# Last projection and final norm in pieces of 384 and 128 tokens, with the final products two tiles at a time

## The chip, the cores and the metric

The kernel runs on one core of one Trainium2 chip. The metric is the device time of one execution in microseconds (us). A core has a matrix engine (PE; its weight loads are shown apart as PEld), a vector engine (DVE), a scalar engine (ACT), a general engine (POOL) and a queue engine (SP) that issues the transfers (DMAs). Each engine runs its own instruction list strictly in order; semaphores join them. Every matmul has its weight load (LDWEIGHTS) ahead of it.

## The reference

A two-layer encoder over 512 tokens with 1024 features, in float32. Layer 0 mixes with differential attention and a gated linear recurrence, layer 1 with a spatial gating unit; each layer ends with a SwiGLU feed-forward. What matters here is the end:

```python
def rms_norm(x, gain):
    xf = x.astype(jnp.float32)
    y = xf * lax.rsqrt(jnp.mean(xf * xf, axis=-1, keepdims=True) + EPS)
    return (y * gain.astype(jnp.float32)).astype(x.dtype)

def swiglu(h, w_in, w_out):
    gate, up = jnp.split(h @ w_in, 2, axis=-1)
    return (jax.nn.silu(gate) * up) @ w_out
...
        h = h + swiglu(rms_norm(h, norm_ffn[l]), w_ffn_in[l], w_ffn_out[l])
    return rms_norm(h, norm_final)
```

## The kernel before, in words

The state `h` lies transposed on the chip: 8 feature tiles of 128 partitions by 512 tokens, two tiles to a buffer (`hs[0]` to `hs[3]`). A product takes its float32 operands as two rounded parts, high and low (type fp32r), and forms three matmuls for each pair of blocks: high by high, high by low, low by high. They accumulate in a PSUM tile of up to 512 tokens.

The program is not written in the order in which it runs. Every step is recorded as an operation with an engine, an estimated cost in us and the buffers that it reads and writes (`Plan.op`, L80). `Plan.schedule` (L110) then plays the whole program through with these costs: whenever an engine is free in that model, it takes the ready operation of lowest priority number for which buffer slots are free. The order of these starts is the order in which instructions are issued on each engine. So a cost that is changed anywhere can move operations anywhere, and on the chip an engine keeps the order even where the real times differ from the costs. `vtt` records a DVE step, `gtt` a POOL step, `act` an ACT step, `mms` a group of matmuls, all through helper lines (L298, L310, L322, L329), so the profile's rows are told apart by their tiles.

The feed-forward (`ffn`, L982) makes 22 gated tiles in groups of 2, 4, 4, 4, 4, 4. `one` (L995) adds the product of one group with the output weights for one feature tile `d`. For all groups but the last of layer 1 it runs over all 512 tokens (tiles `fo_...`). The last group, four tiles (`g18b` and `g20b` hold two each), is projected by the code at the end (L1099 to L1138): a loop `e` over two halves of the tokens, in each a loop over the 8 feature tiles. One pass of the inner loop is 4 x 3 = 12 matmuls into a PSUM tile `last` (there are four such slots), a DVE subtraction into `h` (the weights are laid out so that the product is subtracted), a square on ACT (`sq_fin`), the sum of the first seven squares on POOL, and a scaling of `h` by the gain on ACT. After the 8 tiles, the two squares tiles are summed over the features by matmuls with one column (`st_fin`, plain float32, two rows of the trace for each matmul), DVE forms mean plus epsilon (`ms_fin`), POOL takes the power -1/2 (`rr_fin`), DVE puts that on a diagonal (`dg_fin`), a matmul spreads it over all partitions (`sp_fin`), DVE multiplies each tile of `h` by it, and SP sends the result out in five DMAs for each half.

Earlier in the program the same kind of norm stands in layer 1 (`rstat`, L417; tiles `st_m`, `ms_m`, `rr_m`, `rp_m`, `dg_m`, `sp_m`), between the products `vo` of the spatial gating unit; `wlo` is the low part of a weight tile there.

Of the kernel before, what the change touches and what calls it, by code (L numbers as in the profile page):

```python
# [24 lines left out]
GROUPS = (2, 4, 4, 4, 4, 4)
H = S // 2
# [188 lines left out]
def encoder_kernel(  # L215
# [21 lines left out]
    nc = tc.nc  # L237
    V, A, G, T = nc.vector, nc.scalar, nc.gpsimd, nc.tensor
# [32 lines left out]
    plan = Plan(kinds, limits)  # L271
# [33 lines left out]
    def vts(o, a, s0, s1, op0=ALU.mult, op1=ALU.add, cost=0.07):  # L305
        return plan.op("DVE", cost, lambda: V.tensor_scalar(use(o), use(a), use(s0), use(s1), op0, op1),
                       [o], [a, s0, s1])

    def gtt(o, a, b, op, cost=1.25, prio=None):
        return plan.op("POOL", cost, lambda: G.tensor_tensor(use(o), use(a), use(b), op), [o], [a, b], prio=prio)  # L310
# [8 lines left out]
    def act(o, a, func, scale=1.0, bias=0.0, accum=None, cost=0.52, table=None, prio=None):  # L319
        def fn():  # L320
            kw = {} if accum is None else {"accum_out": use(accum)}
            A.activation(use(o), use(a), func, bias=use(bias), scale=use(scale), **kw)  # L322
        outs = [o] if accum is None else [o, accum]
        return plan.op("ACT", cost, fn, outs, [a, bias, scale], table=table, prio=prio)

    def mms(ps, items, after=(), cost=None):
        def fn():
            for o, l, r, s0, s1 in items:
                T.matmul(use(o), lhsT=use(l), rhs=use(r), start=s0, stop=s1)  # L329
        ins = [x for it in items for x in it[1:3]]  # L330
        return plan.op("PE", cost if cost is not None else 0.2315 * len(items), fn, [ps], ins, after=after)

    colt = cst.tile([P, 50], F32, name="colt")
    ident = cst.tile([P, P], F32, name="ident")
    ones = cst.tile([P, 1], F32, name="ones")
    mhalf = cst.tile([P, NB], F32, name="mhalf")
    onesf = cst.tile([P, P], F32, name="onesf")
# [233 lines left out]
    for i in range(2):  # L571
        ps = buf("aux", f"u{i}")
# [268 lines left out]
    d0 = da_proj(0)  # L841
    gla_core(3, r3, vi)
    d1 = da_proj(1)
# [7 lines left out]
    for h in range(NB):  # L851
        ps = project(we[28 + h], xs0, f"g{h}")
# [8 lines left out]
    hs = [buf("big", f"h{j}") for j in range(KC // 2)]  # L861
# [120 lines left out]
    def ffn(l, norm, name, finish, after=()):  # L982
        gs, k0 = [], 0

        def quad(q, n, k0):
            i = weights[0]
            weights[0] += 1
            pr = -1e6 + i * 10
            raw = buf("hraw", f"raw{i}", shape=(P, 4, n * P))
            off = 4 * P * k0  # L990
            hdma(raw, wfo[l, q, :, off:off + 4 * n * P].rearrange("p (d c) -> p d c", d=4), 256 * n, pr)
            return [rounded(raw(lambda ap, e=e: ap[:, 2 * e:2 * e + 2]), (P, 2, n * P), f"{e}_{i}", pr,
                            lo_cost=0.06 + n * 0.27, hi_cost=0.09 + n * 0.22) for e in range(2)]

        def one(d, wt, ps, n, gs, cols=None):  # L995
            cut = (lambda ap: ap) if cols is None else (lambda ap: ap[:, cols:cols + H])
            o = ps(cut if cols is None else (lambda ap: ap[:, :H]))
            hi, lo = wt
            for k in range(n):
                wh, wl = (b(lambda ap, k=k: blk(ap[:, d % 2], k)) for b in (hi, lo))  # L1000
                xh, xl = (View(g.buf, g.part, lambda ap, g=g: cut(g.fn(ap))) for g in gs[k])
                mms(ps, [(o, wh, xh, k == 0, False), (o, wh, xl, False, False), (o, wl, xh, False, k == n - 1)],
                    cost=0.7 if cols is None else 0.36)

        def out(dp, wts, n, gs, last):
            for d in (2 * dp, 2 * dp + 1):
                ps = buf("aux", f"fo{d}_{k0}{name}")
                one(d, wts, ps, n, gs)
                hd = row(hs[d // 2], d % 2)
                o = vtt(hd, hd, ps, ALU.subtract)  # L1010
                if last:
                    finish(hd)
                    marks.append(o)

        prev, k0 = None, 0
        m = 0
        for gi, n in enumerate(GROUPS):
            cur, store = [], None
            wts = {}
            for i in range(n):  # L1020
                y = gated(l, m, norm, name, after if m < 3 else ())
                if i % 2 == 0:
                    store = buf("huge", f"g{m}{name}", F32R)
                split_pair(store, y, 2 * (i % 2))
                cur.append(pair(store, 2 * (i % 2)))
                m += 1
                if prev:
                    if i % 2 == 0:
                        wts = dict(zip((i, i + 1), quad(i // 2, prev[1], prev[2])))
                    out(i, wts[i], prev[1], prev[0], False)  # L1030
            prev = (cur, n, m - n)
        gs, n, k0 = prev
        wts = quad(0, n, k0) + quad(1, n, k0)
        return gs, n, wts, one, out
# [4 lines left out]
    gs, n, wts, one, out_pair = ffn(0, n1, "a", n2.add, after=[da_end[3]])  # L1039
# [18 lines left out]
    for hf in range(2):  # L1058
        ps = project_natural(wov[hf], n2.xs, f"vo{hf}")
# [17 lines left out]
    for g in range(KC):  # L1077
        ps = project(wo[g], n2.xs, f"uo{g}")
# [13 lines left out]
        b, i = mxs[g - g % 2], 2 * (g % 2)  # L1092
# [5 lines left out]

    fin = [None, None]  # L1099
    gs, n, wts, one, _ = ffn(1, n3, "b", None)  # L1100
    for e in range(2):
        for d in range(KC):
            ps = buf("aux", f"last{d}{e}")
            one(d, wts[d // 2], ps, n, gs, e * H)
            hv = hs[d // 2](lambda ap, d=d, e=e: ap[:, d % 2, e * H:(e + 1) * H], part=(d % 2, e))
            vtt(hv, hv, ps(lambda ap: ap[:, :H]), ALU.subtract, cost=0.34)
            sq = buf("tmp", f"sq_fin{d}{e}")
            sv = sq(lambda ap: ap[:, :H])
            act(sv, hv, AF.Square, cost=0.35)
            if d == 0:  # L1110
                fin[e] = sq
            elif d < KC - 1:
                f = fin[e](lambda ap: ap[:, :H])
                gtt(f, f, sv, ALU.add, cost=0.7)
            act(hv, hv, AF.Copy, scale=colt[:, 4 * KC + d:4 * KC + d + 1], cost=0.4)
        st = buf("aux", f"st_fin{e}")
        for i, x in enumerate((fin[e], sq)):
            for t in range(2):
                mms(st, [(st(lambda ap, t=t: ap[:, t:t + 1]), x(lambda ap, t=t: blk(ap, t)), ones,
                          i == 0 and t == 0, i == 1 and t == 1)], cost=0.28)  # L1120
        ms, rr = buf("ms", f"ms_fin{e}"), buf("rr", f"rr_fin{e}")
        vts(ms(lambda ap: ap[:, 0:2]), st(lambda ap: ap[:, 0:2]), 1.0 / D, EPS)
        gtt(rr(lambda ap: ap[:, 0:2]), ms(lambda ap: ap[:, 0:2]), mhalf[:, 0:2], ALU.pow, cost=0.6)
        dg = buf("trn", f"dg_fin{e}")
        vtt(dg(lambda ap: ap[:, 0, :H].rearrange("p (b c) -> p b c", b=2)),
            ident.rearrange("p (b c) -> p b c", b=1).broadcast_to([P, 2, P]),
            rr(lambda ap: ap[:, 0:2].rearrange("p (b c) -> p b c", c=1).broadcast_to([P, 2, P])), ALU.mult, cost=0.34)
        sp_ = buf("aux", f"sp_fin{e}")
        sv = sp_(lambda ap: ap[:, :H])
        mms(sp_, [(sv, onesf, dg(lambda ap: ap[:, 0, :H]), True, True)], cost=0.45)  # L1130
        for d0, d1 in ((0, 1), (1, 2), (2, 4), (4, 6), (6, 8)):
            j, i, n_ = d0 // 2, d0 % 2, d1 - d0
            for d in range(d0, d1):
                v = hs[d // 2](lambda ap, d=d, e=e: ap[:, d % 2, e * H:(e + 1) * H], part=(d % 2, e))
                vtt(v, v, sv, ALU.mult, cost=0.34)
            plan.op("DMA", n_ * 128 / 360, lambda d0=d0, d1=d1, j=j, i=i, n_=n_, e=e: nc.sync.dma_start(
                out[d0:d1, :, e * H:(e + 1) * H].rearrange("a p c -> p a c"),
                hs[j].ap()[:, i:i + n_, e * H:(e + 1) * H]), [], [hs[j](part=(x, e)) for x in range(i, i + n_)])  # L1138

    with tc.manual_schedule(engines={ENG.PE, ENG.DVE, ENG.Activation, ENG.Pool, ENG.SP}):  # L1140
        for o in plan.schedule():
# [80 lines left out]
```

## Time and profile before

| | |
|---|---|
| median of 3 runs | 1203.88 us (1202.47 to 1203.91) |
| profiled execution, own time | 1204.61 us |
| its span, first to last instruction | 1202.80 us |
| PE busy | 1163.3 us, 97% of the span |
| DVE busy | 915.4 us, 76% |
| ACT busy | 579.1 us, 48% |
| POOL busy | 188.0 us, 16% |
| granted PE clock, mean | 0.995 |

The profile is one execution. Its busy share of PE tells that nearly the whole span is matmuls one behind the other; where something else sets the time is seen by stage, in the chain of waits and in the timeline. A matmul's own duration includes the way through the array, and the next starts before it ends, so what a matmul costs in a stream is the distance between starts.

### The profile page before, as it was taken

How to read it: one execution, taken by the hardware profiler on the slowest of the kernel's cores; microseconds unless marked ns; L12 is line 12 of the kernel's file. 1: busy time of each engine (PE TensorE's matmuls, PEld its weight loads, DVE VectorE, ACT ScalarE, POOL GpSimd, SP SyncE). 2: the span in 40 equal slices, each digit the busy share in tenths (PEclk: the TensorE clock that was granted, in tenths of full speed). 3: DMA queues.
4: the chain of work that ended last, by engine and by line, in shares of the span. 5: the costliest groups of instructions: out<-in, count | busy, mean ns of one | idle time of the engine just before them, and what ended most of it. 6: DMA issues, size and time to landing. Idle time of an engine off the chain costs nothing.

```text
span 1202.8 us, 17650 instructions
## 1 busy us (share of the span) xinstructions
PE 1163.3 (97%) x7072; PEld 1031.0 (86%) x7072; DVE 915.4 (76%) x1304; ACT 579.1 (48%) x881; POOL 188.0 (16%) x185
## 2 busy tenths in 40 slices
PE   6989999999999999999999999999999999999997
PEld 3868888778778999999999888878899999999996
DVE  5467698769697997777777873757799778877874
ACT  5244465657554544444444444335555444444444
POOL 4355584213130000000000040003000000000003
PEclk9989999999999999999999999999999999999998
DMA  6420420343415232424233423330333232323302
GB/s 217 165 82 1 111 81 10 91 123 88 158 35 174 81 106 70 141 71 141 71 140 106 141 78 98 88 105 5 148 110 133 71 132 79 108 102 106 105 1 71
DMA packets 28686, 118.58 MB, mean 99 GB/s; under 512 B 5272, under 2 KB 7448, under 8 KB 20412
## 3 DMA queue, kind: packets, MB, share of 16 engines
q1 hardware_dynamic: 28604, 117.46, 29.5%
q8 instruction: 55, 0.90, 0.3%
q14 instruction: 27, 0.22, 0.1%
HBM read 115.30 MB, written 4.23 MB: 99 GB/s over the span
## 4 chain that ended last, share of the span: by engine, by line
PE 80%; DMA 7%; DVE 6%; issue 4%; ACT 2%; POOL 1%; SPq 0%; POOLq 0%; DVEq 0%; ACTq 0%
PE fo_0b L329 8%; PE fo_0a L329 8%; PE uo L329 4%; PE oo L329 4%; PE vo L329 3%; PE lv L657 2%; DMA raw<-wev 2%; PE fo_18a L329 2%; PE vi L329 2%; PE last L329 1%; PE q L329 1%; PE zf L329 1%; PE zb L329 1%; PE oe L329 1%; DMA xin<-xT 1%
## 5 line engine op out<-in xcount | busy, mean ns | idle before, releaser
L298 DVE TENSOR_TENSOR wlo<-raw,whi 128x1024 fp32r<-128x1024 f32 (+1 forms) x65 | 85.4, 1314 | 29.5 <-ACT whi L317 29.4
L298 DVE TENSOR_TENSOR lb<-comb,hb 128x1024 fp32r<-128x1024 f32 x44 | 53.7, 1220 | 38.5 <-ACT hb L317 38.5
L317 ACT CAST whi<-raw 128x1024 fp32r<-128x1024 f32 (+1 forms) x65 | 66.8, 1031 | 22.3 <-DMA raw<-wev 10.7
L298 DVE TENSOR_TENSOR la<-raw,ha 128x1024 fp32r<-128x1024 f32 x44 | 55.0, 1249 | 27.1 <-ACT ha L317 26.9
L317 ACT CAST hb<-comb 128x1024 fp32r<-128x1024 f32 x44 | 46.1, 1048 | 59.7 <-PE pa9a L948 2.4
L310 POOL TENSOR_TENSOR sq_m<-sq_m,sq_m 128x512 f32<-128x512 f32 x12 | 19.9, 1657 | 328.9 <-ACT sq_m L322 328.4
L317 ACT CAST ha<-raw 128x1024 fp32r<-128x1024 f32 x44 | 46.2, 1049 | 48.8 <-PE pa10a L948 2.4
L298 DVE TENSOR_TENSOR l<-raw,h 128x1024 fp32r<-128x1024 f32 (+1 forms) x48 | 54.5, 1136 | 17.0 <-ACT h L317 15.4
L317 ACT CAST hc<-comb 128x1024 fp32r<-128x1024 f32 x44 | 46.1, 1047 | 37.3 <-PE fo_0b L329 15.5
L298 DVE TENSOR_TENSOR comb<-comb,raw 128x512 f32<-128x512 f32 x88 | 62.4, 709 | 0.1
L317 ACT CAST h<-raw 128x1024 fp32r<-128x1024 f32 (+1 forms) x48 | 46.6, 975 | 27.9 <-PE pb4b L948 2.0
L310 POOL TENSOR_TENSOR sq_fin<-sq_fin,sq_fin 128x256 f32<-128x256 f32 x12 | 8.9, 738 | 327.2 <-ACT sq_fin L322 326.8
L687 POOL TENSOR_TENSOR W<-W,T 128x512 f32<-128x512 f32 x38 | 52.7, 1394 | 39.7 <-PE lv L657 35.5
L298 DVE TENSOR_TENSOR lc<-comb,hc 128x1024 fp32r<-128x1024 f32 x44 | 54.7, 1244 | 2.2 <-ACT hc L317 2.2
L924 DVE TENSOR_TENSOR comb<-raw 128x1024 f32<-128x1024 f32 x44 | 54.7, 1243 | 0.0
L329 PE MATMUL vo<-whi,x_m 128*128 128x512 f32 x128 | 40.3, 391 | 0.1
L329 PE MATMUL uo<-x_m,whi 128*128 128x512 f32 x128 | 40.1, 394 | 0.0
L329 PE MATMUL oo<-mx,whi 128*128 128x512 f32 x128 | 39.6, 390 | 0.0
L657 PEld LDWEIGHTS lv<-W,km 128*128 128x128 f32 x224 | 31.4, 196 | 8.6 <-ACT km L650 6.2
L317 ACT CAST hd<-raw 128x512 fp32r<-128x512 f32 x44 | 27.4, 622 | 22.4 <-PE pa0a L948 2.0
L657 PE MATMUL lv<-W,km 128*128 128x128 f32 x224 | 32.5, 290 | 5.8 <-ACT km L650 5.8
L310 POOL TENSOR_TENSOR sq_f<-sq_f,sq_f 128x512 f32<-128x512 f32 x12 | 20.2, 1686 | 103.1 <-ACT sq_f L322 103.1
(2624 smaller groups left out, 4208.7 us busy)
## 6 DMA issues: line engine op xcount, KB each, us to landing
raw<-wfi SPq DMA_DIRECT2D x44, 1024.0 KB, 4.9
raw<-wfo SPq DMA_DIRECT2D x20, 1024.0 KB, 4.9
raw<-we SPq DMA_DIRECT2D x23, 512.0 KB, 5.2
raw<-wev SPq DMA_DIRECT2D x8, 512.0 KB, 12.4
raw<-woe SPq DMA_DIRECT2D x8, 512.0 KB, 3.8
raw<-wov SPq DMA_DIRECT2D x8, 512.0 KB, 3.7
raw<-wo SPq DMA_DIRECT2D x8, 512.0 KB, 3.6
raw<-woo SPq DMA_DIRECT2D x8, 512.0 KB, 3.7
```

The source lines that it names most:

```text
L298: return plan.op("DVE", cost, lambda: V.tensor_tensor(use(o), use(a), use(b), op), [o], [a, b], prio=prio, after=after, alt=alt, port=insi ...
L310: return plan.op("POOL", cost, lambda: G.tensor_tensor(use(o), use(a), use(b), op), [o], [a, b], prio=prio)
L317: return plan.op("ACT", cost, lambda: A.copy(use(o), use(a)), [o], [a], prio=prio)
L329: T.matmul(use(o), lhsT=use(l), rhs=use(r), start=s0, stop=s1)
L657: T.matmul(blk(ps.ap(), b), lhsT=blk(km.ap(), b), rhs=mixed(0, b * P, P, s)(W.ap()), start=True, stop=True)
L687: return lambda: eng.tensor_tensor(view(W.ap()), view(W.ap()), fn(TT.ap()), ALU.mult)
L924: plan.op("DVE", 1.14, lambda: V.tensor_tensor(comb.ap()[:, 0:2], raw.ap()[:, 0:1].broadcast_to([P, 2, S]), raw.ap()[:, 1:3], ALU.add), [c ...
```

## The change

The two halves become a piece of 384 tokens and a piece of 128 tokens. The squares are summed on DVE and no longer on POOL. The final multiplication takes two feature tiles with one DVE instruction, and the output leaves in four DMAs for each piece in place of five. The costs given to the scheduler become formulas of the width; for the 512-token products of both feed-forwards that gives 0.70072 in place of 0.7 for each block.

```diff
-        def one(d, wt, ps, n, gs, cols=None):
-            cut = (lambda ap: ap) if cols is None else (lambda ap: ap[:, cols:cols + H])
-            o = ps(cut if cols is None else (lambda ap: ap[:, :H]))
+        def one(d, wt, ps, n, gs, c0=0, w=S):
+            cut = lambda ap: ap[:, c0:c0 + w]
+            o = ps(lambda ap: ap[:, :w])
...
-                    cost=0.7 if cols is None else 0.36)
+                    cost=0.03 + w * 0.00131)
...
-    for e in range(2):
+    for e, (c0, w) in enumerate(((0, 3 * P), (3 * P, P))):
+        nb = w // P
+        cw = lambda ap, w=w: ap[:, :w]
         for d in range(KC):
             ps = buf("aux", f"last{d}{e}")
-            one(d, wts[d // 2], ps, n, gs, e * H)
-            hv = hs[d // 2](lambda ap, d=d, e=e: ap[:, d % 2, e * H:(e + 1) * H], part=(d % 2, e))
-            vtt(hv, hv, ps(lambda ap: ap[:, :H]), ALU.subtract, cost=0.34)
+            one(d, wts[d // 2], ps, n, gs, c0, w)
+            hv = hs[d // 2](lambda ap, d=d, c0=c0, w=w: ap[:, d % 2, c0:c0 + w], part=(d % 2, e))
+            vtt(hv, hv, ps(cw), ALU.subtract, cost=0.06 + w * 0.00105)
...
             elif d < KC - 1:
-                f = fin[e](lambda ap: ap[:, :H])
-                gtt(f, f, sv, ALU.add, cost=0.7)
-            act(hv, hv, AF.Copy, scale=colt[:, 4 * KC + d:4 * KC + d + 1], cost=0.4)
+                f = fin[e](cw)
+                vtt(f, f, sv, ALU.add, cost=0.06 + w * 0.00105)
+            act(hv, hv, AF.Copy, scale=colt[:, 4 * KC + d:4 * KC + d + 1], cost=0.2 + w * 0.0008)
         st = buf("aux", f"st_fin{e}")
         for i, x in enumerate((fin[e], sq)):
-            for t in range(2):
+            for t in range(nb):
...
-        for d0, d1 in ((0, 1), (1, 2), (2, 4), (4, 6), (6, 8)):
-            j, i, n_ = d0 // 2, d0 % 2, d1 - d0
-            for d in range(d0, d1):
-                v = hs[d // 2](lambda ap, d=d, e=e: ap[:, d % 2, e * H:(e + 1) * H], part=(d % 2, e))
-                vtt(v, v, sv, ALU.mult, cost=0.34)
-            plan.op("DMA", n_ * 128 / 360, lambda d0=d0, d1=d1, j=j, i=i, n_=n_, e=e: nc.sync.dma_start(
-                out[d0:d1, :, e * H:(e + 1) * H].rearrange("a p c -> p a c"),
-                hs[j].ap()[:, i:i + n_, e * H:(e + 1) * H]), [], [hs[j](part=(x, e)) for x in range(i, i + n_)])
+        for j in range(KC // 2):
+            v = lambda ap, c0=c0, w=w: ap[:, :, c0:c0 + w]
+            plan.op("DVE", 0.06 + w * 0.0021, lambda j=j, v=v, sp_=sp_, w=w: V.tensor_tensor(
+                v(hs[j].ap()), v(hs[j].ap()),
+                sp_.ap()[:, :w].rearrange("p (a c) -> p a c", a=1).broadcast_to([P, 2, w]), ALU.mult),
+                [hs[j](part=(x, e)) for x in range(2)], [sp_], prio=1e6 + len(plan.ops))
+            plan.op("DMA", w / 360, lambda j=j, v=v, c0=c0, w=w: nc.sync.dma_start(
+                out[2 * j:2 * j + 2, :, c0:c0 + w].rearrange("a p c -> p a c"), v(hs[j].ap())),
+                [], [hs[j](part=(x, e)) for x in range(2)])
```

What stands where now, at the places that the prediction speaks of. In these rows the number behind a tile's name tells buffers apart; `h_2550`, `h_2562`, `h_2573` and `h_2587` are `hs[0]` to `hs[3]`.

On DVE, the end of the second half before, from the subtraction of the last tile (`last_11050`) to the multiplications:

```order
L298 TENSOR_TENSOR h_2587<-h_2587,last_11032 128x256
L298 TENSOR_TENSOR h_2587<-h_2587,last_11050 128x256
L306 TENSOR_SCALAR ms_fin_11079<-st_fin_11073 128x2
L298 TENSOR_TENSOR dg_fin_11083<-ident,rr_fin_11081 128x256
L298 TENSOR_TENSOR h_2550<-h_2550,sp_fin_11085 128x256 x2
```

The same place now; `sp_fin_10974` belongs to the piece of 384, the other tiles to the piece of 128, whose last subtraction is that of `last_11038`:

```order
L298 TENSOR_TENSOR h_2587<-h_2587,last_11019 128x128
L298 TENSOR_TENSOR h_2587<-h_2587,last_11038 128x128
L298 TENSOR_TENSOR sq_fin_10944<-sq_fin_10944,sq_fin_11047 128x128
L1136 TENSOR_TENSOR h_2587<-h_2587,sp_fin_10974 128x2x384
L298 TENSOR_TENSOR sq_fin_10944<-sq_fin_10944,sq_fin_11062 128x128
L306 TENSOR_SCALAR ms_fin_11074<-st_fin_11071 128x1
L298 TENSOR_TENSOR dg_fin_11078<-ident,rr_fin_11076 128x128
L1136 TENSOR_TENSOR h_2550<-h_2550,sp_fin_11080 128x2x128
```

Between the last subtraction and the statistics DVE now has three instructions, one of them a product of the other piece with 768 elements in each partition.

On PE, in the first tiles of the last projection before: the first matmul that reads the second pair of `g20b` is that of `last_10754` in the last row, behind the second and third block of the fourth tile, `last_10792`.

```order
L329 MATMUL last_10792<-g18b,h_130_10714 128x256 x2
L329 MATMUL last_10792<-g18b,l_130_10728 128x256
L329 MATMUL last_10792<-g20b,h_130_10714 128x256 x2
L329 MATMUL last_10792<-g20b,l_130_10728 128x256
L329 MATMUL last_10754<-g20b,h_130_10676 128x256 x2
```

The same place now:

```order
L329 MATMUL last_10794<-g18b,h_130_10714 128x384 x2
L329 MATMUL last_10794<-g18b,l_130_10728 128x384
L329 MATMUL last_10754<-g20b,h_130_10676 128x384 x2
L329 MATMUL last_10754<-g20b,l_130_10691 128x384
L329 MATMUL last_10770<-g20b,h_130_10676 128x384 x2
```

Ahead of that matmul stood 36 of 256 tokens, three blocks for each of four tiles; now there are 30 of 384 tokens, since the fourth tile has only one block there.

On DVE in the norm of layer 1, between the products `vo` (minus before, plus now):

```order
-L306 TENSOR_SCALAR ms_m_6528<-st_m_6518 128x4
-L298 TENSOR_TENSOR wlo_6535<-raw_6436,whi_6523 128x1024
-L428 CAST rp_m_6546<-rr_m_6530 128x4
-L298 TENSOR_TENSOR rp_m_6546<-rr_m_6530,rp_m_6546 128x4
-L298 TENSOR_TENSOR dg_m_6551<-ident,rp_m_6546 128x512 x2
+L306 TENSOR_SCALAR ms_m_6523<-st_m_6515 128x4
+L428 CAST rp_m_6535<-rr_m_6525 128x4
+L298 TENSOR_TENSOR wlo_6540<-raw_6436,whi_6530 128x1024
+L298 TENSOR_TENSOR rp_m_6535<-rr_m_6525,rp_m_6535 128x4
+L298 TENSOR_TENSOR dg_m_6546<-ident,rp_m_6535 128x512 x2
```

The weight step `wlo` has gone behind the first step that needs POOL's result. On PE both groups of that norm, `st_m` and `sp_m`, stand three `vo` matmuls earlier than before. Up to there, and between there and the end of the program, the instructions on every engine stand as before.

## Rows read from the trace of the kernel before

**Rows 1.** Chain of waits, 1150 to 1203 us: start, us, what, rows merged
```profile
1163.46 4.12 PE fo_0b L329 x18
...
1172.14 8.41 PE last L329 x68
1180.55 0.78 PE st_fin L329 x8
1181.34 2.26 PE last L329 x18
1183.60 0.43 PE sp_fin L329 x2
1184.03 6.84 PE last L329 x57
```

**Rows 2.** Timeline behind the last projection: start, us, engine, line, what, [idle before <- releaser]
```profile
1192.01 0.28 PE L329 MATMUL last<-g20b,l 128*128 128x256 f32 x1
1192.33 0.42 DVE L298 TENSOR_TENSOR h<-h,last 128x256 f32<-128x256 f32 x1 [1.02 <-PE last L329]
1192.69 1.17 PE L329 MATMUL st_fin<-ones,sq_fin 128*128 128x1 f32 x8 [0.40 <-POOL sq_fin L310]
1192.79 0.42 ACT L322 ACTIVATE sq_fin<-h 128x256 f32<-128x256 f32 x1 [0.48 <-DVE h L298]
1193.90 0.16 DVE L306 TENSOR_SCALAR ms_fin<-st_fin 128x2 f32<-128x2 f32 x1 [1.15 <-PE st_fin L329]
1194.14 0.71 POOL L310 TENSOR_TENSOR rr_fin<-ms_fin,mhalf 128x2 f32<-128x2 f32 x1 [1.50 <-DVE ms_fin L306]
1194.88 0.42 DVE L298 TENSOR_TENSOR dg_fin<-ident,rr_fin 128x256 f32<-128x256 f32 x1 [0.82 <-POOL rr_fin L310]
1195.36 0.70 PE L329 MATMUL sp_fin<-dg_fin,onesf 128*128 128x256 f32 x2 [1.50 <-DVE dg_fin L298]
1196.16 2.74 DVE L298 TENSOR_TENSOR h<-h,sp_fin 128x256 f32<-128x256 f32 x8 [0.86 <-PE sp_fin L329]
```

**Rows 3.** Output DMAs from 1196 us: count, KB each, median us to landing
```profile
outT<-h SPq DMA_DIRECT2D x3, 256.0 KB, 2.7
outT<-h SPq DMA_DIRECT2D x2, 128.0 KB, 1.7
```

**Rows 4.** Issues of line L1136, and DMA by stretch (last two columns: share, GB/s)
```profile
L1136 SPq DMA_DIRECT2D outT<-h x10: 344/380/423, 1184.6 to 1199.1; - x10
...
1199.00:1199.50 0.50, 0.00 (x0) 0.00 (x0) 0.00 (x0) 0.00 (x0) 0.00 (x0) 0.50 1.03 346
```

**Rows 5.** PE timeline, products of 512 tokens: every third row
```profile
1163.77 0.39 PE L329 MATMUL fo_0b<-g16b,l 128*128 128x512 f32 x1
...
1167.18 0.39 PE L329 MATMUL fo_0b<-g16b,l 128*128 128x512 f32 x1
```

**Rows 6.** Plain float32 matmuls of 128 columns and one: timeline, weight loads by tile
```profile
756.74 1.05 PE L329 MATMUL mix<-sgwt,vg 128*128 128x128 f32 x8
...
1180.27 0.98 PEld L329 LDWEIGHTS st_fin<-ones,sq_fin 128*128 128x128 f32 x8
...
L329 PE MATMUL mix<-sgwt,vg x64: 270/275/275, 756.7 to 797.9; 128*128 128x128 f32 x64
...
L329 PEld LDWEIGHTS mix<-sgwt,vg x64: 187/192/192, 756.5 to 797.8; 128*128 128x128 f32 x64
...
L329 PEld LDWEIGHTS last<-g20b,h x64: 186/192/192, 1168.0 to 1191.8; 128*128 128x128 f32 x64
```

**Rows 7.** DVE and POOL groups from 1160 us: count, busy us, mean ns, idle before
```profile
L298 DVE TENSOR_TENSOR l<-raw,h 128x1024 fp32r<-128x1024 f32 x4 | 4.9, 1223 | 3.6 <-ACT h L317 3.6
L298 DVE TENSOR_TENSOR h<-h,fo_0b 128x512 f32<-128x512 f32 x2 | 1.4, 686 | 1.1 <-PE fo_0b L329 1.1
L298 DVE TENSOR_TENSOR h<-h,sp_fin 128x256 f32<-128x256 f32 x16 | 5.5, 415 | 1.3 <-PE sp_fin L329 1.3
L310 POOL TENSOR_TENSOR sq_fin<-sq_fin,sq_fin 128x256 f32<-128x256 f32 x12 | 8.9, 738 | 327.2 <-ACT sq_fin L322 326.8
```

**Rows 8.** Weight loads at 1172 us: the wait inside the first tiles
```profile
1172.13 0.19 PEld L329 LDWEIGHTS last<-g20b,h 128*128 128x128 f32 x1 [0.34 <-DVE g20b L298]
```

**Rows 9.** The norm of layer 1: timeline, and POOL's step by tile
```profile
709.81 0.68 DVE L298 TENSOR_TENSOR sq_m<-sq_m,sq_m 128x512 f32<-128x512 f32 x1
712.72 0.95 PE L329 MATMUL st_m<-ones,sq_m 128*128 128x1 f32 x8
...
713.95 1.97 POOL L310 TENSOR_TENSOR rr_m<-ms_m,mhalf 128x4 f32<-128x4 f32 x1 [5.80 <-DVE ms_m L306]
716.23 1.29 DVE L298 TENSOR_TENSOR dg_m<-ident,rp_m 128x512 fp32r<-128x512 f32 x2
718.39 0.64 PE L329 MATMUL sp_m<-dg_m,onesr 128*128 128x512 f32 x2
...
L310 POOL TENSOR_TENSOR rr_m<-ms_m,mhalf x2: 1032/1500/1969, 34.6 to 713.9; 128x4 f32<-128x4 f32 x2
```

More of the change, by code (lines that the diff above doesn't have):

```diff
@@ L1100, in encoder_kernel @@
     gs, n, wts, one, _ = ffn(1, n3, "b", None)
-    for e in range(2):
+    for e, (c0, w) in enumerate(((0, 3 * P), (3 * P, P))):
+        nb = w // P
+        cw = lambda ap, w=w: ap[:, :w]
         for d in range(KC):
             ps = buf("aux", f"last{d}{e}")
-            one(d, wts[d // 2], ps, n, gs, e * H)
-            hv = hs[d // 2](lambda ap, d=d, e=e: ap[:, d % 2, e * H:(e + 1) * H], part=(d % 2, e))
-            vtt(hv, hv, ps(lambda ap: ap[:, :H]), ALU.subtract, cost=0.34)
+            one(d, wts[d // 2], ps, n, gs, c0, w)
+            hv = hs[d // 2](lambda ap, d=d, c0=c0, w=w: ap[:, d % 2, c0:c0 + w], part=(d % 2, e))
+            vtt(hv, hv, ps(cw), ALU.subtract, cost=0.06 + w * 0.00105)
             sq = buf("tmp", f"sq_fin{d}{e}")
-            sv = sq(lambda ap: ap[:, :H])
-            act(sv, hv, AF.Square, cost=0.35)
+            sv = sq(cw)
+            act(sv, hv, AF.Square, cost=0.15 + w * 0.0007)
             if d == 0:
@@ L1119, in encoder_kernel @@
                 mms(st, [(st(lambda ap, t=t: ap[:, t:t + 1]), x(lambda ap, t=t: blk(ap, t)), ones,
-                          i == 0 and t == 0, i == 1 and t == 1)], cost=0.28)
+                          i == 0 and t == 0, i == 1 and t == nb - 1)], cost=0.38)
         ms, rr = buf("ms", f"ms_fin{e}"), buf("rr", f"rr_fin{e}")
-        vts(ms(lambda ap: ap[:, 0:2]), st(lambda ap: ap[:, 0:2]), 1.0 / D, EPS)
-        gtt(rr(lambda ap: ap[:, 0:2]), ms(lambda ap: ap[:, 0:2]), mhalf[:, 0:2], ALU.pow, cost=0.6)
+        cb = lambda ap, nb=nb: ap[:, 0:nb]
@@ L1124, in encoder_kernel @@
+        vts(ms(cb), st(cb), 1.0 / D, EPS)
+        gtt(rr(cb), ms(cb), mhalf[:, 0:nb], ALU.pow, cost=0.6)
         dg = buf("trn", f"dg_fin{e}")
-        vtt(dg(lambda ap: ap[:, 0, :H].rearrange("p (b c) -> p b c", b=2)),
-            ident.rearrange("p (b c) -> p b c", b=1).broadcast_to([P, 2, P]),
-            rr(lambda ap: ap[:, 0:2].rearrange("p (b c) -> p b c", c=1).broadcast_to([P, 2, P])), ALU.mult, cost=0.34)
+        vtt(dg(lambda ap, w=w, nb=nb: ap[:, 0, :w].rearrange("p (b c) -> p b c", b=nb)),
+            ident.rearrange("p (b c) -> p b c", b=1).broadcast_to([P, nb, P]),
+            rr(lambda ap, nb=nb: ap[:, 0:nb].rearrange("p (b c) -> p b c", c=1).broadcast_to([P, nb, P])),
+            ALU.mult, cost=0.06 + w * 0.00105)
@@ L1128, in encoder_kernel @@
         sp_ = buf("aux", f"sp_fin{e}")
-        sv = sp_(lambda ap: ap[:, :H])
-        mms(sp_, [(sv, onesf, dg(lambda ap: ap[:, 0, :H]), True, True)], cost=0.45)
-        for d0, d1 in ((0, 1), (1, 2), (2, 4), (4, 6), (6, 8)):
-            j, i, n_ = d0 // 2, d0 % 2, d1 - d0
-            for d in range(d0, d1):
-                v = hs[d // 2](lambda ap, d=d, e=e: ap[:, d % 2, e * H:(e + 1) * H], part=(d % 2, e))
-                vtt(v, v, sv, ALU.mult, cost=0.34)
-            plan.op("DMA", n_ * 128 / 360, lambda d0=d0, d1=d1, j=j, i=i, n_=n_, e=e: nc.sync.dma_start(
-                out[d0:d1, :, e * H:(e + 1) * H].rearrange("a p c -> p a c"),
-                hs[j].ap()[:, i:i + n_, e * H:(e + 1) * H]), [], [hs[j](part=(x, e)) for x in range(i, i + n_)])
+        mms(sp_, [(sp_(cw), onesf, dg(lambda ap, w=w: ap[:, 0, :w]), True, True)], cost=0.1 + w * 0.0017)
```

## The prediction

> **What bounds the kernel now.** I read the page's shares first: PE is busy nearly all the span, so I looked for the places where it isn't. The chain of waits over the last 50 us shows PE alone, one matmul behind the other, through the whole last projection [rows 1]: 57 matmuls of 256 tokens in 6.84 us, which is 0.120 us each. Then the timeline behind the last matmul [rows 2] shows a serial tail: the last product ends, DVE subtracts at 1192.33, ACT squares, PE sums, DVE, POOL, DVE, PE, and from 1196.16 eight multiplications on DVE until 1198.90. Last come the output DMAs [rows 3, 4]; the last one is issued at 1199.1 and lands 2.7 us later, near 1201.8, and the span ends at 1202.80, 1.0 us after that. So from the last subtraction's start the tail takes 1202.80 - 1192.33 = 10.47 us, and ahead of it every PE start counts. The change adds or takes on both sides of that border: the width of 192 matmuls ahead of it, and the tail behind.
>
> **PE, ahead of the tail.** 192 matmuls of 256 tokens become 96 of 384 and 96 of 128. The streamed tokens are the same; what matters is the start distance at each width.
>
> 256 tokens: 0.120 us, as above. 512 tokens: 15 starts from 1163.77 to 1167.18 are 0.2273 us each [rows 5]. 384 lies between them, halfway: 0.1737 us.
>
> 128 tokens in fp32r stands nowhere in the trace, so I bound it. From below, the straight line through the two known widths: 0.120 - (0.2273 - 0.120)/2 = 0.066 us. From above, a whole plain float32 product of 128 columns: it takes two rows of the trace, and eight such rows start within 1.05 - 0.275 = 0.775 us for seven distances, 0.111 us a row, 0.222 us a product [rows 6]. In between stands the weight load, which every matmul has of its own: eight loads for matmuls of a single column take 0.98 us, (0.98 - 0.192)/7 = 0.113 us apart [rows 6]. One column and 128 columns have the same distance, so the load paces both. Is the load of an fp32r weight as long? Its row lasts 192 ns in the last projection and 192 ns under `mix`, the float32 case [rows 6]. At 256 tokens the distance of 0.120 us leaves such a load hidden; at 128 tokens it would stick out. I take 0.111 us, the row it is nearest to.
>
> That gives 96 x (0.1737 + 0.111 - 2 x 0.120) = +4.3 us; with the lower bound 0.0 us, with the upper +15.0 us.
>
> Here a rule speaks the other way. The Trainium skill, "TensorE: Matmul & The Clock Gate", section "Back-to-back issue gap", has a sustained 81 ns for each matmul of 128 columns with its weight load; the section "Weight-path perf modes" says that weights are read faster where their type is not FP32. If fp32r counts as "not FP32", its load would be shorter than that of float32; the equal 192 ns rows of this trace speak against that. By 81 ns the term would be +1.4 us instead of +4.3.
>
> Three small PE terms. The first piece's statistics come from 3 + 3 one-column matmuls in place of 2 + 2, so 12 rows for 8, at 0.113: +0.45 us. The spreading matmul of the first piece grows from 256 to 384 columns: its two rows took 0.43 us on the chain [rows 1], half as much again is +0.21 us. The wait of 0.34 us for the second pair of `g20b` [rows 8] goes, since 30 x 0.1737 = 5.2 us of products stand ahead of that matmul where 36 x 0.120 = 4.3 us stood: -0.34 us; nothing else is late there, as the next thing read, the weights of later tiles, is needed later than before. Sum on PE: 4.3 + 0.45 + 0.21 - 0.34 = **+4.6 us**.
>
> **The tail.** DVE durations by size [rows 7]: 1024 elements 1.22, 512 0.686, 256 0.415; that is about 0.00105 us an element, so 0.28 us at 128 and 0.95 at 768. In a row the next starts sooner: eight in 2.74 us are (2.74 - 0.415)/7 = 0.332 apart, 0.08 less than the duration [rows 2]. Now, from the start of the last subtraction:
> - DVE's order puts three instructions between it and the statistics: 0.20 (subtraction) + 0.20 (a sum of squares) + 0.87 (the 768-element product of the other piece) + 0.28 (the last sum) = 1.55 us. The chain through ACT's square would have been ready after about 0.65. The order was made with 0.066 us for a matmul of 128; on the chip DVE will have stood idle before, but can't take the 768 elements earlier.
> - statistics matmuls, four rows as before: ACT's square ended at 1193.21, `ms_fin` started at 1193.90: 0.69.
> - `ms_fin`, POOL's power, to `dg_fin`: 1194.88 - 1193.90 = 0.98.
> - `dg_fin` and `sp_fin` took 1196.16 - 1194.88 = 1.28 at 256 columns; at 128 DVE saves 0.14 and the two matmul rows some 0.2: 0.94.
> - four multiplications of 256 elements: 3 x 0.332 + 0.415 = 1.41 in place of 2.74.
> - the last DMA: issued 0.2 after DVE's end. Before, its 2.7 us to landing held a queue: the DMA engines were full at 346 GB/s [rows 4] with 1 MB of the half. Now it is 128 KB behind three others like it, which is nearer to the two DMAs of that size with 1.7 us [rows 3]. I take 2.0, plus 1.0 to the end: 3.2; bounds 1.7 and 2.7.
>
> Sum: 1.55 + 0.69 + 0.98 + 0.94 + 1.41 + 3.2 = 8.8 us against 10.47: **-1.7 us** (-2.0 to -1.0 by the DMA's bounds).
>
> **What is hidden.** The sums of squares that leave POOL (12 of 738 ns [rows 7]) cost DVE some 0.47 us each in the first piece. There a tile takes PE 12 x 0.1737 = 2.08 us, and DVE has two such instructions in it; in the second piece DVE has 8 subtractions, 6 sums and 4 products of 768, about 6.5 us beside 96 x 0.111 = 10.7 us of PE. Without that cover (PE at 0.066) the leftover would join the tail, a few tenths. What stays is only the order, counted above. SP issues 8 DMAs for 10; the first piece's last, 384 KB, starts behind the product at +1.3 us, needs 1.1 us at 346 GB/s and is out before the second piece's first at about +4.7.
>
> The norm of layer 1 is reordered too. `st_m` comes three products (0.68 us) earlier, near 712.04; its last input ended at 710.49 [rows 9], so it doesn't wait. `sp_m` would start near 717.7 in place of 718.39. Its input: POOL's power took 1.97 us beside a DVE weight step, 1.03 in the other norm [rows 9], and now DVE waits for it; after it come 1.2 of weight step and 1.5 of small steps, so the input is ready between 717.1 and 718.1: a wait of 0 to 0.4 us. I take 0, since DVE stands still beside POOL now.
>
> **Sum.** +4.6 - 1.7 = +2.9 us. The profiled execution took 1204.61, 0.73 above the median of the runs, so it would be 1207.5 there and 1203.88 + 2.9 = **1206.8 us** as a median.
>
> **Rivals.**
> 1. The weight load does not pace 128 tokens, and the distance falls with the width to 0.066. For it: from 512 to 256 tokens it did. Then PE pays only the small terms (+0.3), the tail gives its 1.7 less 0.2 of DVE work left over: -1.2 us, 1202.7. The place is the second piece, the price 96 x the distance, and the point is 0.081 us: below that the kernel is not slower; from 0.105 us on it is slower by over 0.2%. The Trainium skill's 81 ns (the section on the issue gap) lies just at that point and would give about 1204.
> 2. A matmul of 128 fp32r columns costs as much as the float32 one, 0.222 us. For it: no fp32r product under 256 columns stands in the trace to rule it out. Against: at 256 and 512 tokens no such cost shows. Then 15.0 + 0.3 - 1.7 = +13.6 us, 1217.5.
> 3. The tail doesn't shrink as reckoned, the DMA landing at its 2.7: +3.6, 1207.5, which lies inside the forecast's own range.
>
> **How the numbers follow.** Forecast (with rival 3) 0.70, rival 1 0.16, rival 2 0.12, something else 0.02. The forecast's own range takes the distance from 0.104 to 0.120 (+3.6 to +5.2), the tail from -2.0 to -1.0 and up to 0.4 from layer 1: about 1205.8 to 1209.2. To hold 8 in 10 it reaches down into rival 1: 1202.3 to 1209.6; rival 2 is left out. About 0.2%, 2.4 us, is what a measurement of this kernel can tell from no change. Slower: three quarters of the forecast (0.50) and rival 2, 0.62. Same: the rest of the forecast and most of rival 1, 0.33. Faster: 0.05.
>
> **What would show it.** Start distances of the `last` matmuls: 0.174 at 384 and 0.111 at 128 tokens (0.066 and 0.222 are the rivals). The stage from the first `last` start to the last longer by 4.6 us, with no wait for `g20b`. Behind the last matmul the 768-element product on DVE ahead of the statistics, the multiplications starting 4.2 us after the last subtraction started (3.83 before), and a tail of 8.8 us. If the tail were under 8 us, or the 128-token distance under 0.10, the forecast would be wrong.

## The result, and the profile after

The changed kernel takes 1207.53 us (median of 22 runs, 1202.97 to 1217.28), the kernel before 1202.76 us (22 runs beside it, 1201.74 to 1205.56). The ratio is 1.0055, 95% interval [1.0036, 1.0074]: slower, by more than 0.2%. The times of the changed kernel fall into two groups: 15 executions from 1202.97 to 1210.09 us with a mean granted clock of 0.990 to 0.995 (mean time 1206.67), and 7 from 1214.73 to 1217.28 us with 0.983 to 0.986 (mean 1216.44). The kernel before has one group (mean 1203.15). So the difference of the means, 6.6 us, is 3.5 us that every execution pays and 7/22 x 9.8 = 3.1 us from the second group. The profiled execution is of the first group: 1206.9 us, span 1205.1.

First the border of the stage. In the kernel before, the first product of the last projection starts here (PE timeline):

```profile
1167.41 0.40 PE L329 MATMUL last<-g18b,h 128*128 128x256 f32 x2
```

The same timeline after:

```profile
1166.44 0.51 PE L329 MATMUL last<-g18b,h 128*128 128x384 f32 x2
...
1182.94 0.33 PE L329 MATMUL last<-g20b,l 128*128 128x384 f32 x1
1183.11 0.33 PE L329 MATMUL last<-g18b,h 128*128 128x128 f32 x2
...
1183.73 0.78 PE L329 MATMUL st_fin<-ones,sq_fin 128*128 128x1 f32 x6
1184.37 0.42 PE L329 MATMUL last<-g20b,h 128*128 128x128 f32 x2
...
1184.73 0.78 PE L329 MATMUL st_fin<-ones,sq_fin 128*128 128x1 f32 x6
1185.37 0.42 PE L329 MATMUL last<-g20b,h 128*128 128x128 f32 x2
...
1189.09 0.86 PE L329 MATMUL sp_fin<-dg_fin,onesf 128*128 128x384 f32 x2
1189.49 0.63 PE L329 MATMUL last<-g20b,h 128*128 128x128 f32 x2
1189.96 0.27 PE L329 MATMUL last<-g20b,l 128*128 128x128 f32 x1
...
1190.29 0.28 PE L329 MATMUL last<-g20b,l 128*128 128x128 f32 x1
...
1190.63 0.28 PE L329 MATMUL last<-g18b,l 128*128 128x128 f32 x1
...
1190.96 0.28 PE L329 MATMUL last<-g18b,l 128*128 128x128 f32 x1
```

The 96 starts of 384 tokens lie between 1166.44 and 1183.11: 0.1736 us each. In the piece of 128, every third row is shown from 1190.29 on: 0.67 us for six starts, 0.112 each. The statistics rows take 0.64 us twice, and the spreading matmul 0.40 plus 0.25 that the next three products start late, in all 0.65.

Then the tail, in the timeline that answers to [rows 2]:

```profile
1195.96 0.29 DVE L298 TENSOR_TENSOR h<-h,last 128x128 f32<-128x128 f32 x1 [1.05 <-PE last L329]
1196.17 0.28 DVE L298 TENSOR_TENSOR sq_fin<-sq_fin,sq_fin 128x128 f32<-128x128 f32 x1
1196.29 0.31 ACT L322 ACTIVATE sq_fin<-h 128x128 f32<-128x128 f32 x1 [1.03 <-DVE h L298]
1196.37 0.95 DVE L1136 TENSOR_TENSOR h<-h,sp_fin 128x768 f32<-128x768 f32 x1
1197.23 0.28 DVE L298 TENSOR_TENSOR sq_fin<-sq_fin,sq_fin 128x128 f32<-128x128 f32 x1
1197.58 0.61 PE L329 MATMUL st_fin<-ones,sq_fin 128*128 128x1 f32 x4 [1.65 <-DVE sq_fin L298]
1198.22 0.16 DVE L306 TENSOR_SCALAR ms_fin<-st_fin 128x1 f32<-128x1 f32 x1 [0.70 <-PE st_fin L329]
1199.04 0.29 DVE L298 TENSOR_TENSOR dg_fin<-ident,rr_fin 128x128 f32<-128x128 f32 x1 [0.66 <-POOL rr_fin L310]
1199.38 0.80 PE L329 MATMUL sp_fin<-dg_fin,onesf 128*128 128x128 f32 x2 [1.20 <-DVE dg_fin L298]
1200.22 1.42 DVE L1136 TENSOR_TENSOR h<-h,sp_fin 128x256 f32<-128x256 f32 x4 [0.89 <-PE sp_fin L329]
```

The stretch of its span from 1199.4 to 1200.0 us, in which the spreading matmul runs (columns: stretch, us, busy time and count for PE, PEld, DVE, ACT, POOL, then the granted clock, DMA share and GB/s):

```profile
1199.40:1200.00 0.60, 0.60 (x2) 0.48 (x2) 0.00 (x0) 0.00 (x0) 0.00 (x0) 0.50 0.01 3
```

And the output DMAs from 1184 us, which answer to [rows 3] (count, KB each, median us to landing):

```profile
outT<-h SPq DMA_DIRECT2D x4, 384.0 KB, 2.5
outT<-h SPq DMA_DIRECT2D x4, 128.0 KB, 1.9
```

Their issues, which answer to [rows 4] (duration in ns: lowest, median, highest; start of the first and the last):

```profile
L1140 SPq DMA_DIRECT2D outT<-h x8: 372/397/451, 1191.0 to 1202.2; - x8
```

The last subtraction starts at 1195.96, so the stage takes 29.52 us where it took 1192.33 - 1167.41 = 24.92: +4.60. The tail takes 1205.1 - 1195.96 = 9.14 us for 10.47: -1.33. Together that is +3.27, beside the 3.5 that the runs of the first group show. The two profiled spans differ by 2.3 only, because in this execution the stage happened to begin 0.97 us earlier, at 1166.44. In the traces of all the kernels here that start lies between 1161.76 and 1167.41 us, a spread of over 5 us ahead of everything that the last projection does.

### The profile page after: what moved, and what is told of

Its sections match the earlier page's. It is cut to its first block, busy times and chain, and to the rows that moved or that the text cites. A ratio compares the mean times of both kernels' runs of the same rounds, so it can differ in the third digit from the quotient of the medians.

```text
span 1205.1 us, 17624 instructions
## 1 busy us (share of the span) xinstructions
PE 1168.3 (97%) x7072; PEld 1036.4 (86%) x7072; DVE 919.8 (76%) x1308; ACT 579.6 (48%) x881; POOL 178.4 (15%) x173
## 4 chain that ended last, share of the span: by engine, by line
PE 79%; DMA 7%; DVE 5%; issue 5%; ACT 2%; POOL 1%; SPq 0%; POOLq 0%; DVEq 0%; ACTq 0%
PE fo_0b L329 8%; PE fo_0a L329 8%; PE uo L329 4%; PE oo L329 4%; PE vo L329 3%; PE lv L657 2%; DMA raw<-wev 2%; PE fo_18a L329 2%; PE vi L329 2%; PE last L329 1%; PE q L329 1%; PE zf L329 1%; PE oe L329 1%; PE zb L329 1%; DMA xin<-xT 1%
## 5 line engine op out<-in xcount | busy, mean ns | idle before, releaser
L310 POOL TENSOR_TENSOR sq_f<-sq_f,sq_f 128x512 f32<-128x512 f32 x12 | 20.2, 1684 | 103.1 <-ACT sq_f L322 103.1
```

## The experiments

The theory: the weight load paces products of 128 tokens at 0.111 us, which costs +4.6 us on PE, and the shorter tail gives back less than 2 us. The rivals of the prediction were a distance that falls with the width, or a float32 price. What had to be added was the question why some executions take 10 us more. The kernel before was measured again beside each group of runs, on the same chip, and the ratios are against that (one execution of it of 1280 us, beside the first four runs, is left out).

**The widths alone.** In the kernel before, only the pieces; sums on POOL, products tile by tile and five DMAs stay. The costs given to the scheduler for the steps of the pieces follow the widths.

```diff
...
-    for e in range(2):
+    for e, (c0, w) in enumerate(((0, 3 * P), (3 * P, P))):
...
```

> Only the widths are changed to 384 and 128 tokens; sums of squares stay on POOL, multiplications tile by tile, five DMAs a piece, and the layer-1 norm keeps its old order. If the weight load that paces 128 tokens is the cause: start distances 0.173 and 0.111 us, the stage from the first product to the last subtraction about 29.5 us (24.9 before), a tail near 8.5 us, time about +2.5 to +4 us in most executions. If the other parts of the change cost the time: within 1 us of before. On the executions at 1215 to 1217 us: if the PE clock falls in the stretch of 128 tokens, some show here too; if they come from the reordered norm of layer 1, none.

Ratio 1.0096 [1.0074, 1.0117], 6 runs from 1207.5 to 1214.33 us, five of them over 1210, with mean clocks of 0.983 to 0.986. The sixth (0.991) is at 1207.5, still 6.7 above the mean of the kernel before; +2.5 to +4 was expected of most. The profiled one (1214.33 us) caught what the profile above did not. The stretches of its span, with the same columns as above:

```profile
1180.00:1185.00 5.00, 5.00 (x40) 5.00 (x39) 1.56 (x4) 2.74 (x6) 1.39 (x2) 1.00 0.01 3
1185.00:1190.00 5.00, 5.00 (x28) 5.00 (x27) 1.04 (x3) 1.01 (x4) 1.31 (x2) 0.54 0.00 0
1190.00:1195.00 5.00, 5.00 (x21) 4.39 (x21) 2.27 (x5) 0.45 (x2) 0.45 (x1) 0.50 0.16 59
```

And its PE timeline just ahead of the fall:

```profile
1182.06 0.33 PE L329 MATMUL last<-g18b,h 128*128 128x128 f32 x2
...
1183.35 1.44 PE L329 MATMUL st_fin<-ones,sq_fin 128*128 128x1 f32 x12
1184.65 0.42 PE L329 MATMUL last<-g18b,h 128*128 128x128 f32 x2
...
1185.92 0.63 PE L329 MATMUL last<-g20b,h 128*128 128x128 f32 x2
...
1187.20 0.63 PE L329 MATMUL last<-g18b,h 128*128 128x128 f32 x2
```

PE never stands still (5.00 of 5.00), yet at about 1185.4 us, in the narrow piece and some 0.6 us behind the end of the twelve one-column rows (1183.35 + 1.44 = 1184.79), the granted clock falls from 1.00 to 0.50, from 2.4 to 1.2 GHz, and stays there. Six starts then take 1.28 us (1185.92 to 1187.20), 0.213 each, and so on to the end of the piece.

**Everything but the widths.** The changed kernel with two halves.

```diff
-    for e, (c0, w) in enumerate(((0, 3 * P), (3 * P, P))):
+    for e, (c0, w) in enumerate(((0, 2 * P), (2 * P, 2 * P))):
```

> Two halves of 256 tokens, all other parts of the change kept (sums on DVE, two tiles at a time, four DMAs, the reordered norm of layer 1). If the widths are the cause: PE stage as before (24.9 us, less the 0.0 to 0.4 us of waits), tail 10 to 10.5 us, time within 0.7 us of before. If the other parts are the cause: +2 us or more. Executions above 1214 us: none if the clock falls in the stretch of 128 tokens, some if the reordered norm of layer 1 is behind them.

Ratio 1.0009 [0.9996, 1.0021], 12 runs from 1200.2 to 1204.03 us, one group. The sums on DVE, the two-tile products, the four DMAs and the moved norm of layer 1 change nothing that can be measured. The loss is the widths'.

**Four pieces of 128.**

```diff
...
-    for e, (c0, w) in enumerate(((0, 3 * P), (3 * P, P))):
+    for e, (c0, w) in enumerate(((0, P), (P, P), (2 * P, P), (3 * P, P))):
```

> Four pieces of 128 tokens: the suspected cost four times over the tokens. If the weight load paces 128 tokens: 384 products at 0.111 us are 42.6 us for 23.0, so +19.6 us, +2 to +3 for the statistics of more pieces, tail as with the change (-1.3): about 1222 to 1225 us with the PE clock full throughout. If the distance fell with the width (0.066): 25.3 us, about 1205. If the clock falls in such a stretch, most executions show it, and the time goes up to 20 us beyond that.

Ratio 1.0168 [1.0147, 1.0189], 4 runs from 1219.98 to 1222.88 us. Its chain of waits has 66 products in one row:

```profile
1193.32 7.32 PE last L329 x66
```

That is 0.111 us each at a granted clock of 1.00, and 384 x 0.111 - 192 x 0.120 = +19.6 us is nearly the whole loss, 20.2 us between the means. The clock did not fall, in some 45 us of such products with two or four one-column rows at a time. So in these four executions narrow products alone did not bring it down.

**64 columns at a time.** In the changed kernel each product of 128 tokens is done as two of 64.

```diff
...
+                if w == P:
+                    for q in range(2):
+                        oq = ps(lambda ap, q=q: ap[:, q * 64:q * 64 + 64])
...
```

> As the change, but each product of the 128-token piece is done as two of 64 columns, each with its own weight load. If the load paces: 192 distances of 0.111 for 96, +10.7 us on the change, about 1218 us, and rows of 64 columns 0.111 apart. If 0.111 us came from the columns: 0.056 apart, the time that of the change.

Ratio 1.0270 [1.0249, 1.0292], 4 runs from 1231.59 to 1234.86 us. Its PE timeline:

```profile
1179.57 0.28 PE L329 MATMUL last<-g18b,l 128*128 128x64 f32 x1
...
1179.90 0.28 PE L329 MATMUL last<-g18b,l 128*128 128x64 f32 x1
...
1182.02 1.28 PE L329 MATMUL st_fin<-ones,sq_fin 128*128 128x1 f32 x6
...
1201.51 0.40 PE L329 MATMUL last<-g18b,l 128*128 128x64 f32 x1
...
1202.15 0.40 PE L329 MATMUL last<-g18b,l 128*128 128x64 f32 x1
```

At full clock three products of 64 columns take 0.33 us, 0.11 each: as long as 128 columns. Half the columns buy nothing: the price goes with the number of products, each with its weight load, and not with the columns. That it is the load, and no other fixed price of such a pair, is how it is read here; no run has a product without a load. From 1182.5 us on the granted clock is 0.50, and three take 0.64 us, again as with 128 columns. Here all four runs have a low mean clock (0.973 to 0.978), which the expected 1218 us left out.

**The planner's cost.** Three products of 128 tokens take 0.34 us, and the change tells the planner 0.03 + 128 x 0.00131 = 0.198.

```diff
-                    cost=0.03 + w * 0.00131)
+                    cost=0.34 if w == P else 0.03 + w * 0.00131)
```

> The change, with the scheduler told 0.34 us for three products of 128 tokens (0.113 each) in place of 0.198. DVE then does the last 768-element product ahead of the last subtraction. If the order on DVE is the cause of the long way to the statistics: multiplications start 3.2 us after the last subtraction started (4.26 with the change), tail 8.2 us for 9.1, time 0.9 us below the change where the clock stays full. If the way through ACT and PE was late anyway: no gain. The PE stage stays at 29.5 us by both. The clock should still fall in some executions.

Ratio 1.0069 [1.0046, 1.0093], 12 runs: three from 1200.87 to 1204.52 us (clock 0.994), nine from 1211.39 to 1215.67 (clock 0.981 to 0.988). In the timeline of the tail no other step of DVE stands between the subtraction and the statistics any more:

```profile
1201.81 0.29 DVE L298 TENSOR_TENSOR h<-h,last 128x128 f32<-128x128 f32 x1 [1.60 <-PE last L329]
...
1203.11 0.16 DVE L306 TENSOR_SCALAR ms_fin<-st_fin 128x1 f32<-128x1 f32 x1 [1.02 <-PE st_fin L329]
...
1205.11 1.42 DVE L1136 TENSOR_TENSOR h<-h,sp_fin 128x256 f32<-128x256 f32 x4 [0.89 <-PE sp_fin L329]
```

The multiplications start 3.30 us after the last subtraction, for 4.26 above, with 0.80 us for the spreading matmul in both: the order on DVE cost 0.96 us. The gain drowns in the executions at half clock.

**A second piece of 256 columns.** The second piece multiplies 256 tokens and uses the last 128; the other 128 are worked out for nothing.

```diff
...
-            one(d, wts[d // 2], ps, n, gs, c0, w)
+            one(d, wts[d // 2], ps, n, gs, min(c0, 2 * P), max(w, 2 * P))
...
```

> The change, with the products of the second piece 256 tokens wide, of which 128 are computed twice and not used. If 128 tokens are paced by the weight load, 256 cost nearly the same: 96 x (0.120 - 0.111) = +0.9 us on the PE stage; if the distance went with the columns, +5 us and more. If the half clock comes from the weak use of the columns in this stretch, no execution shows it here: all between 1.002 and 1.005 of before; if it comes from anything else in this piece (the statistics' matmuls, the transfers), some lie 9 to 10 us higher.

Ratio 1.0023 [1.0011, 1.0035], 12 runs from 1200.92 to 1207.24 us, one group. Twice the columns in the second piece are hardly dearer than 128 (0.120 us for 0.112, 0.8 us in all), the planner's order comes right (multiplications 2.86 us after the last subtraction), and in the trace the clock keeps 1.00 through the piece with the same twelve one-column rows in it.

**The statistics with 128 columns.** In the kernel with the widths alone, the statistics matmuls stream 128 columns of ones in place of one; one column of the result is read.

```diff
...
-                mms(st, [(st(lambda ap, t=t: ap[:, t:t + 1]), x(lambda ap, t=t: blk(ap, t)), ones,
+                mms(st, [(st(lambda ap, t=t: blk(ap, t)), x(lambda ap, t=t: blk(ap, t)), onesf,
...
```

> As e1_width (widths of the change alone), but the statistics' matmuls have 128 columns of ones in place of one, which by the load's pace costs nothing. In e1_width the clock fell to half in 5 of 6 executions, in the one profiled 2 us after twelve one-column rows that stood in a row behind the first 128-token products; with four pieces of 128 tokens, where only two such rows stand together, it never fell. If the one-column rows are what makes it fall: full clock in all or nearly all executions, time near +3 us on before. If products of 128 tokens alone do it: as e1_width, most executions near +13.

Ratio 1.0033 [1.0021, 1.0045], 12 runs from 1202.76 to 1208.88 us, mean clock 0.988 to 0.996 in all, one group. Without this edit, on another chip, five of six were over 1210 at 0.986 or less. The mean does not tell a late fall, though: in the profiled execution (0.992) the clock falls too, at about 1192.0 us, with the last three products. Ahead of that its chain shows a wait that doesn't belong to the question: the eight separate products of the first piece on DVE hold up a PSUM slot.

```profile
1185.70 3.82 DVE h L298 x8
1189.52 0.04 issue
1189.56 1.57 PE last L329 x12
```

PE stands still for 1.00 us of it, from the end of its products at 1188.56 on.

**The changed kernel again**, beside the last three.

> The changed kernel again, on the chip of these experiments. By the load's pace +2.5 to +4 us on before where the clock stays full. In about a third of the executions 9 to 10 us more; if the profile falls on one of these, its clock should fall to 0.5 between the start of the 128-token piece and its middle and stay there, products 0.213 us apart.

Ratio 1.0055 [1.0027, 1.0082], 8 runs: five from 1202.59 to 1207.91 us, three from 1212.9 to 1215.43. The two groups are there again. Its profiled execution, of the first group, has the stage and the tail of the one above: 29.52 us (1162.13 to 1191.65) and 9.15.

**Both mendings, and a control.** The changed kernel with the planner's cost of 0.34 and statistics of 128 columns; beside it, on the same chip, the one with the cost alone.

> The changed kernel with two edits: the statistics products take 128 columns of ones in place of one (all columns of the result are alike, the first is read on), and the planner is given 0.34 us for three products of 128 tokens, as they take, so that VectorE does the first piece's last multiplication ahead of the last subtraction. Theory (one-column rows inside the 128-token piece are what let the granted clock fall; the products of 128 cost 0.111 us for the weight load at full clock): no execution falls to half clock in the piece, so all stay within 1200 to 1209 us, 128-token products 0.111 us apart, about 3.3 us from the last subtraction to the first multiplication; PE +4.6 and tail -2.3 give +2.3 us on before, ratio 1.000 to 1.004. Rival (the fall comes from the load-paced 128-token products themselves or from chance): a third or more of the executions lie 10 us higher, at 1211 to 1216, as the same kernel with one-column rows does beside it.

> The changed kernel with the planner's cost of three products of 128 tokens at 0.34 us alone, the statistics rows with one column as before: the control for the run beside it, on the same chip. Theory: some of the executions, from a third to three quarters, fall to half clock in the 128-token piece and end at 1211 to 1216 us, the rest at 1200 to 1206. Rival (chance or another chip's habit made the half-clock executions of the earlier run): none or one of them lies above 1210.

With both: ratio 1.0015 [1.0003, 1.0027], 12 runs from 1201.99 to 1205.66 us with a mean clock of 0.991 to 0.996, none in a second group. The control: 1.0046 [1.0021, 1.0071]; one execution of 4059 us aside, six of eleven have a mean clock of 0.981 to 0.986 and take 1210.05 to 1214.96 us, the other five (0.994) 1200.95 to 1206.23. The control's timeline shows the fall itself:

```profile
1186.36 0.27 PE L329 MATMUL last<-g18b,l 128*128 128x128 f32 x1
1186.46 0.39 PE L329 MATMUL last<-g18b,h 128*128 128x128 f32 x2
1186.69 0.31 PE L329 MATMUL last<-g18b,l 128*128 128x128 f32 x1
1186.80 0.63 PE L329 MATMUL last<-g20b,h 128*128 128x128 f32 x2
1187.23 0.42 PE L329 MATMUL last<-g20b,l 128*128 128x128 f32 x1
...
1187.87 0.41 PE L329 MATMUL last<-g20b,l 128*128 128x128 f32 x1
```

Up to 1186.69 three starts take 0.33 us, from 1187.23 on 0.64. With both edits the narrow piece, from 1179.49 us on, keeps the clock until the last products, and PE first stands still behind them; its later stretches:

```profile
1185.00:1190.00 5.00, 5.00 (x47) 5.00 (x47) 4.57 (x10) 2.00 (x6) 0.00 (x0) 1.00 0.63 234
1190.00:1195.00 5.00, 3.35 (x27) 2.97 (x27) 1.89 (x8) 2.25 (x7) 0.55 (x1) 1.00 0.22 81
```

Its tail, in the timeline:

```profile
1192.48 0.29 DVE L298 TENSOR_TENSOR h<-h,last 128x128 f32<-128x128 f32 x1 [0.39 <-PE last L329]
...
1194.86 0.49 PE L329 MATMUL sp_fin<-dg_fin,onesf 128*128 128x128 f32 x2 [1.21 <-DVE dg_fin L298]
1195.38 1.41 DVE L1137 TENSOR_TENSOR h<-h,sp_fin 128x256 f32<-128x256 f32 x4 [0.58 <-PE sp_fin L329]
```

The multiplications start 2.90 us after the last subtraction, and with the clock still at 1.00 the spreading matmul takes 0.49 us for 0.80. The span ends at 1200.2, so the tail is 7.72 us, 2.75 less than before. The stage takes 29.65 us (1162.83 to 1192.48), +4.73, and that leaves +2.0; the means differ by 1.6 (1203.79 and 1202.22). This is the best form with a narrow piece that was run, and it does not beat the kernel before.

## Why the prediction was right, and where it was not

The sign and the mechanism held, and the size for the executions at full clock. One cost was not foreseen at all, and that the median came so near is partly luck.

- *The distance at 128 tokens*, the step on which the most hung, was taken as 0.111 us from the weight loads of one-column matmuls [rows 6]. It measured 0.112 (and 0.111 over 66 products of the four pieces). That 64 columns take as long shows that it is not the columns that set it. Rival 1, a distance that falls with the width, and rival 2, 0.222 us, are both out: below 0.081 it would have paid. The 81 ns of the Trainium skill ("TensorE: Matmul & The Clock Gate", "Back-to-back issue gap") does not hold for these fp32r products with a load each.
- *384 tokens* at 0.1737: measured 0.1736. *The small PE terms*: 12 statistics rows 1.28 us for 0.78, +0.50 (+0.45 forecast). The spreading matmul is 0.65 us (0.64 forecast), no wait for `g20b` [rows 8] is left. The whole stage: +4.60, forecast +4.6.
- *The tail*: forecast 8.8, measured 9.14. The order on DVE stood as read: subtraction to statistics 1.62 us (1.55), and the cost experiment shows 0.96 us of it as lost. The multiplications start 4.26 us after the subtraction (4.2). Three steps were mis-sized. `ms_fin` to `dg_fin` took 0.82 us, not 0.98: POOL's power took 0.55 us for 0.71 [rows 2]. `dg_fin` to the multiplications took 1.18 us, not 0.94: I let the spreading matmul shrink with its columns, but it took 0.80 us for 0.70 [rows 2]: by the stretch shown above the granted clock was 0.50 there, after PE had mostly stood still since the last product, while with both mendings the clock was still 1.00 and it took 0.49 us. From the end of the multiplications to the end of the span it took 3.46, not 3.2. The DMAs landed in 1.9 us, near the 2.0 that was taken, but the last was issued at 1202.2, 0.56 us behind DVE's end (1201.64) and not 0.2: the four issues of the piece start 0.5 us apart, 1200.7 to 1202.2, while the products on DVE follow each other at 0.333.
- *The norm of layer 1 at nothing*: everything but the widths, with that reorder in it, measured 1.0009 [0.9996, 1.0021]. In the trace of the changed kernel PE does not wait for `sp_m`, which starts at 716.82 us, 5.68 behind `st_m`.
- *What failed*: the step that took PE at full clock through the whole second piece. Nothing in the prediction speaks of the clock there, and all that it had not named had a chance of 0.02. In 7 of 22 executions and 3 of 8, by their mean clock, it falls to half, and the 96 products pay 0.213 for 0.112 from there on; if 78 of them are left, as in the control's trace, that is 78 x 0.101 = 7.9 of the 9.8 us between the groups. In that trace the stage takes 38.25 us and the tail 8.24, for 29.65 and 7.72 with both mendings: 9.1 us in all.
- *The luck*: the forecast of 1206.8 us stands on the first three runs of the kernel before, with a median of 1203.88; beside the change that kernel had 1202.76. Against that the median moved by 4.8 us and the mean by 6.6, not by 2.9. The part of the cost that was not foreseen was in part made up by a start 1.1 us too high. The first group alone moved by 3.5.
- *A slip*: the bounds of the own range give 1203.88 + 5.2 + 0.3 - 1.0 + 0.4 = 1208.8 us at its upper end, not 1209.2.

That the runs of the second group are those of the half clock is inferred from traces of two sister kernels (three executions), not of the changed kernel itself, whose two profiled executions were both of the first group. For it there is the mean clock: 0.983 to 0.986 against 0.990 to 0.995, and 78 products at half clock, 16.6 us, take 0.5 x 16.6/1205 = 0.007 off the mean.

## What to carry to other kernels

Before making the last piece narrow, find the width below which a product with its weight load costs the same however few columns it has (here between 256 and 128): below it half the columns save nothing, and a shorter tail has to pay for that with every product of the piece. When a planner orders the work, give it the measured distance of the narrow products and not a line through wider ones, or the engine beside PE is put in the wrong order just where the tail begins. A stretch that PE fills without a gap can still lose half its clock, as the pieces of 128 and 64 columns did here, so look at the granted clock in several executions before trusting one.

## What the runs showed of the hardware

The granted clock of PE fell from 1.00 to 0.50 while PE stood still for nothing: with the widths alone, 5.00 us of work in every 5.00 us on either side of the fall. The Trainium skill ("TensorE: Matmul & The Clock Gate", "HAM oscillation — how this bites in real kernels") gives idle gaps of PE as what brings the clock down; no such gap stands ahead of the fall in the four traces that have it early in the piece (the widths alone, 64 columns, the planner's cost twice). What PE did before it fell was products of 128 or 64 columns at 0.111 us each, with twelve one-column rows among them (with 64 columns it fell as the second six of them began).

By time and mean clock, no execution of 24 fell early in the piece with 128 columns in those twelve rows, and 30 of 59 did with one column (the widths alone 5 of 6, the changed kernel 7 of 22 and 3 of 8, the planner's cost 9 of 12 and 6 of 11). With products of 64 columns 4 of 4 did, with 256 columns none of 12, and in four pieces of 128 with fewer such rows together none of 4. Whether an execution falls is decided by something that these runs don't show; that the one-column rows tip it is shown by the pair on one chip, six of eleven against none of twelve.

The weight load follows the clock: in the control's trace its row lasts 0.19 us at full clock and 0.33 at half, and the pace of the products goes from 0.111 to 0.213 us.
